# Staging four channels of both halves in two idle store tiles of a sliding-window kernel

## The chip, the cores and the metric

The kernel runs on one core of a Trainium2 chip. The metric is the device time of one execution in microseconds (us). All data is float32. The core has 16 DMA engines; DMAs are issued from the queues of SP (SyncE), ScalarE (ACT in the profile) and GpSimd (POOL in the profile). VectorE is DVE.

## The reference

The input x has shape (16, 64, 64, 64): batch, channel, row, column. The window is 8 by 8 with a stride of 4, so there are 15 by 15 windows. Each is cut out of all 64 channels:

```python
for i in range(n_h):                  # 15
    for j in range(n_w):              # 15
        result[:, i, j] = x[:, :, 4*i : 4*i + 8, 4*j : 4*j + 8]
```

The result has shape (16, 15, 15, 64, 8, 8). It is 58.98 MB, against 16.78 MB of input; nothing is computed, only copied.

## The kernel before, in words

**The input tile L.** The whole input lies in SBUF in one tile L of 128 partitions x (32 channels x 16 rows x 64 columns), 128 KB a partition. A partition is 64 * ch + 4 * b + q: half of the channels ch (0 or 1), batch b, row group q of 16 rows. One (channel, row group) of one batch is 4 KB in a row in memory. Partitions are also spoken of by y, the half of the batch: y = 0 is batches 0 to 7.

**The loads (L56 to L117).** `load(eng, ch, y, q, c0, c1)` fetches channels c0 to c1 of one half for one row group of eight batches: eight partitions, four apart, one 4 KB piece for each channel. The loop over y and q (eight steps) issues:

- on SP, first-half channels 4 to 32 for all eight steps (`HWP` = 8), each cut in two DMAs for the first five (`TWICE` = 5): 13 DMAs;
- on POOL, first-half channels 0 to 4 (`SMALL` = 4), then the second half, channels 0 to 32, or 8 to 32 where q = 0: 16 DMAs.

Ahead of the loop ScalarE issues one load (L106) of 16 partitions, all batches of q = 0: second-half channels 0 to 8 (`EC`).

**The index tiles (L69 to L101).** POOL and VectorE compute small tiles idx, idx_hi, idx_lo, idx_y with the row of the output that each partition goes to; this is over at 3.7 us.

**The store tiles.** Four tiles G0 to G3 of 128 partitions x 16 KB are used in turn (`tile_`). A partition of such a tile is one whole window: 64 channels x 8 x 8. Copies on ScalarE and VectorE gather windows out of L into a tile, then POOL issues an indirect DMA (`scatter`, L131) that writes 128 windows, 16 KB each, to their places in the output. Rows that fall outside are dropped by the bounds check.

- `part` (L182, copies in L189) fills a tile from one y alone, so it can start when half of the batches are loaded: eight copies of 32 partitions x 2048 elements. The first three tiles of the kernel are parts of y = 0, into G0, G1, G2.
- Then three parts of y = 1 alternate with `unit`s, which take both y and fill 64 partitions by each copy.
- `unit` with s > 0 makes windows that cross two row groups. There VectorE shifts the lower rows by one partition with a shuffle (L154).
- The last column is stored by two plain DMAs from SP (L238) out of partitions 32 to 96 of two tiles.

Waits between engines and the order of instructions on each engine are set by the framework from the data that they touch. In the program the loads stand ahead of all copies.

Of the kernel before, what the change touches and what calls it, by code (L numbers as in the profile page):

```python
# [10 lines left out]
def kernel(  # L11
# [7 lines left out]
    nc = tc.nc  # L19
    P = nc.NUM_PARTITIONS  # L20

    B, C, H, W = x.shape
    Bo, NH, NW, Co, WSo, WSo2 = out.shape
    WS = int(window_size)
# [3 lines left out]
    f32 = mybir.dt.float32  # L28
    i32 = mybir.dt.int32
    ALU = mybir.AluOpType  # L30
    CH = 2
    HQ = P // (B * CH)
    CL = C // CH
    RB = H // HQ
# [3 lines left out]
    HP = P // CH  # L38
    YB = 8
    NY = B // YB  # L40
    QP = YB * HQ
# [4 lines left out]
    gpool = ctx.enter_context(tc.tile_pool(name="gpool", bufs=1))  # L46


    L = lpool.tile([P, CL, RB, W], f32)
# [1 line left out]

    SMALL, HWP, TWICE = 4, 8, 5

    def load(eng, ch, y, q, c0, c1):  # L56
        p0 = ch * HP + y * QP + q
        eng.dma_start(out=L[p0 : p0 + QP - HQ + 1 : HQ, c0:c1, :, :], in_=x_v[ch, y, q, :, c0:c1, :])  # L58
# [42 lines left out]
    tt(idx_lo, idx_lo, th, ALU.add)  # L101


    EC = 8
    x_b = x.rearrange("b (ch cl) (hq r) w -> ch hq b cl (r w)", ch=CH, hq=HQ)
    nc.scalar.dma_start(out=L[HP : HP + (B - 1) * HQ + 1 : HQ, 0:EC, :, :], in_=x_b[1, 0, :, 0:EC, :])  # L106

    for y in range(NY):
        for q in range(HQ):
            hw = y * HQ + q < HWP  # L110
            if hw:
                mid = (SMALL + CL) // 2 if y * HQ + q < TWICE else CL
                load(nc.sync, 0, y, q, SMALL, mid)
                if mid < CL:
                    load(nc.sync, 0, y, q, mid, CL)
            load(nc.gpsimd, 0, y, q, 0, SMALL if hw else CL)
            load(nc.gpsimd, 1, y, q, EC if q == 0 else 0, CL)  # L117

    o_v = out.rearrange("b i j c r w -> (b i j) (c r w)")
    nxt = [min(p + 1, 31) for p in range(32)]  # L120
    NG = 4
    G = [gpool.tile([P, C, WS, WS], f32, name=f"G{n}") for n in range(NG)]

    o_q = out.rearrange("b i j c r w -> i j b (c r w)")

# [51 lines left out]
    def tile_():  # L177
        nonlocal at
        at += 1
        return G[(at - 1) % NG]  # L180

# [46 lines left out]
    for s in range(2):  # L228
        g = tile_()
        cols = slice(j * ST, j * ST + WS)  # L230
        for y in range(NY):
            d = slice(QP + y * QP, QP + (y + 1) * QP)
            for ch in range(CH):
                f = slice(ch * HP + y * QP, ch * HP + (y + 1) * QP)
# [39 lines left out]
```

## Time and profile before

| | |
|---|---|
| median of 3 runs | 188.5 us (188.49 to 189.4) |
| the profiled execution | 189.08 us, span 187.3 us |
| busy: VectorE, ScalarE, POOL | 142.5 us (76%), 139.3 us (74%), 45.0 us (24%) |
| DMA | 75.81 MB, mean 405 GB/s |
| queues' share of the 16 engines' time | POOL 84.6%, SP 12.8%, ScalarE 1.1% |
| HBM | 16.78 MB read, 62.91 MB written |

The span is the profiled execution from its first to its last instruction; the time of the run is 1.8 us longer. In the profile a line such as L189 is a line of the kernel's file; `G<-L` names what is written and read. The page's slices divide the span in 40 equal parts of 4.68 us; a DMA digit is the mean busy share of the 16 engines in tenths. Queue q0 is POOL's, q1 SP's, q10 ScalarE's. The "HBM written" counts also the rows that the bounds check drops; the DMA total does not.

### The profile page before, as it was taken

The page shows a single profiled execution, that of the slowest core. Times are in us where ns is not written, and L with a number is a line of the kernel's source. Part 1 is how long each engine was busy: PE and PEld are TensorE (multiplying, and loading weights), DVE is VectorE, ACT ScalarE, POOL GpSimd, SP SyncE. Part 2 cuts the span into 40 slices and gives each one's busy share as a digit, 9 for nine tenths or more (in the row PEclk, how much of TensorE's full clock was granted, in tenths as well). Part 3 has the DMA queues.
Part 4 walks back from the last instruction along what each step waited for, and adds up shares of the span by engine and source line. Part 5 has one row for each costly group of instructions (what it writes and reads, how often), then busy time and mean ns, then how long its engine had stood idle before and what let it go on. Part 6 is the DMA issues. An engine that isn't in the chain of part 4 may idle for free.

```text
span 187.3 us, 567 instructions
## 1 busy us (share of the span) xinstructions
DVE 142.5 (76%) x203; ACT 139.3 (74%) x94; POOL 45.0 (24%) x50
## 2 busy tenths in 40 slices
DVE  5000009998597969799999999999999999999600
ACT  0000009998599979988899999998999899989700
POOL 7411222207207050501222222112211121113000
DMA  5999999999999999999999999999999999999994
GB/s 127 295 402 400 400 400 398 399 400 419 421 427 437 425 427 423 441 413 434 434 420 432 422 434 413 441 430 420 434 416 436 406 437 409 420 423 406 441 420 206
DMA packets 10988, 75.81 MB, mean 405 GB/s; under 512 B 3288, under 2 KB 3288, under 8 KB 7384
## 3 DMA queue, kind: packets, MB, share of 16 engines
q0 software_dynamic: 8784, 65.81, 84.6%
q1 hardware_dynamic: 2056, 9.44, 12.8%
q10 hardware_dynamic: 144, 0.52, 1.1%
q14 instruction: 4, 0.03, 0.0%
HBM read 16.78 MB, written 62.91 MB: 425 GB/s over the span
## 4 chain that ended last, share of the span: by engine, by line
DMA 53%; DVE 28%; issue 6%; ACT 5%; POOL 2%; ACTq 1%; DVEq 0%; PEldq 0%
DMA L<-in_x_dram 20%; DMA out_dram<-G,idx_y 14%; DVE G L161 14%; DMA out_dram<-G,idx 13%; DVE G L154 9%; DMA out_dram<-G,idx_lo 6%; DVE G L189 4%; ACT G L236 3%; POOL L L58 2%; ACT G L151 1%; ACT G L165 1%; ACTq L269 1%; DVE G L151 0%; POOL pi L69 0%; DVEq L161 0%
## 5 line engine op out<-in xcount | busy, mean ns | idle before, releaser
L151 ACT COPY G<-L 64x2048 f32<-64x2048 f32 x46 | 87.2, 1896 | 5.1 <-DMA out_dram<-G,idx 2.9
L189 DVE COPY G<-L 32x2048 f32<-32x2048 f32 x30 | 36.7, 1224 | 29.9 <-DMA L<-in_x_dram 24.1
L161 DVE STREAM_SHUFFLE G<-L 64x1024 f32<-64x1024 f32 (+4 forms) x39 | 53.0, 1360 | 1.3
L154 DVE STREAM_SHUFFLE G<-L 64x1024 f32<-64x1024 f32 x30 | 38.4, 1281 | 0.0
L189 ACT COPY G<-L 32x2048 f32<-32x2048 f32 x18 | 33.9, 1896 | 4.1 <-DMA L<-in_x_dram 2.8
L189 ACT ACT_TABLE_LOAD x1 | 1.3, 1283 | 27.7 <-DMA L<-in_x_dram 27.7
L131 POOL DMA_INDIRECT out_dram<-G,idx_y x6 | 10.0, 1664 | 28.4 <-DVE G L189 27.4
L58 POOL DMA_DIRECT2D L<-in_x_dram x16 | 11.0, 700 | 22.2 <-DMA L<-in_x_dram 21.7
L131 POOL DMA_INDIRECT out_dram<-G,idx_lo x8 | 7.7, 961 | 30.6 <-DVE G L154 26.9
L131 POOL DMA_INDIRECT out_dram<-G,idx x8 | 9.2, 1152 | 17.8 <-DVE G L161 6.8
L131 POOL DMA_INDIRECT out_dram<-G,idx_hi x7 | 6.7, 960 | 27.0 <-DVE G L154 19.0
L165 ACT COPY G<-L 64x256 f32<-64x256 f32 (+2 forms) x21 | 10.2, 484 | 0.5
L151 DVE COPY G<-L 64x2048 f32<-64x2048 f32 x6 | 7.3, 1222 | 0.2
L236 ACT COPY G<-L 32x768 f32<-32x768 f32 x8 | 6.6, 830 | 0.1
L236 DVE COPY G<-L 32x1280 f32<-32x1280 f32 x8 | 6.5, 818 | 0.1
L161 DVE LOAD_MASK_SELECT G<-L x39 | 0.3, 9 | 1.2 <-DMA out_dram<-G,idx_y 0.9
L72 DVE TENSOR_SCALAR tb<-pi 128x1 int32<-128x1 int32 x1 | 0.2, 155 | 1.0 <-POOL pi L69 1.0
L166 DVE COPY G<-L 64x1280 f32<-64x1280 f32 x1 | 0.9, 876 | 0.0
L78 DVE TENSOR_TENSOR th<-tc,tq 128x1 int32<-128x1 int32 x2 | 0.3, 156 | 0.0
L75 DVE TENSOR_SCALAR th<-tc 128x1 int32<-128x1 int32 x2 | 0.3, 154 | 0.0
L69 POOL IOTA pi<- 128x1 int32 x1 | 0.1, 124 | 0.4 <-PEq L269 0.4
L78 DVE CUSTOM_DVE_ANT_0 idx<-tb,th 128x2 uint16<-128x2 uint16 x1 | 0.2, 160 | 0.0
(19 smaller groups left out, 2.7 us busy)
## 6 DMA issues: line engine op xcount, KB each, us to landing
L<-in_x_dram POOLq DMA_DIRECT2D x6, 1024.0 KB, 21.6
L<-in_x_dram SPq DMA_DIRECT2D x10, 448.0 KB
L<-in_x_dram SPq DMA_DIRECT2D x3, 896.0 KB
out_dram<-G SPq DMA_DIRECT2D x2, 1024.0 KB
L<-in_x_dram POOLq DMA_DIRECT2D x2, 768.0 KB, 17.9
L<-in_x_dram POOLq DMA_DIRECT2D x8, 128.0 KB, 21.5
L<-in_x_dram ACTq DMA_DIRECT2D x1, 512.0 KB
out_dram<-G,idx POOLq DMA_INDIRECT x8, 12.8
```

What stands on the lines that cost most here:

```text
L58: eng.dma_start(out=L[p0 : p0 + QP - HQ + 1 : HQ, c0:c1, :, :], in_=x_v[ch, y, q, :, c0:c1, :])
L75: nc.vector.tensor_scalar(out=d[:, :], in0=a[:, :], scalar1=float(m), scalar2=None, op0=ALU.mult)
L78: nc.vector.tensor_tensor(out=d[:, :], in0=a[:, :], in1=b[:, :], op=op)
L131: st = nc.gpsimd.indirect_dma_start(out=o_v, out_offset=bass.IndirectOffsetOnAxis(ap=ix[:, 0:1], axis=0), in_=g.rearrange("p c r w -> p (c ...
L151: copy(out=g[d, cs, :, :], in_=L[f, :, s * ST : s * ST + WS, cols])
L154: nc.vector.stream_shuffle(out=g[d, cs, ST:WS, :], in_=L[f, :, 0:ST, cols], mask=nxt)
L161: nc.vector.stream_shuffle(out=out, in_=in_, mask=same)
L165: act(out=out[:, 0:k], in_=in_[:, 0:k])
L166: other(out=out[:, k:], in_=in_[:, k:])
L189: (act if (2 * d + ch) % 3 == 0 else dve)(out=g[d * QP : (d + 1) * QP, ch * CL : (ch + 1) * CL, :, :], in_=L[f : f + QP, :, s * ST : s * S ...
L236: copy(out=g[d, ch * CL + c0 : ch * CL + c1, :, :], in_=L[f, c0:c1, s * ST : s * ST + WS, cols])
L269: with _tile.TileContext(nc) as tc:
```

## The change

Four channels (`FC` = 4) of both halves no longer go straight into L. A store tile's 16 KB a partition hold just four channels of 16 x 64 elements, and G2 and G3 are not used as store tiles at first, so they are viewed as staging tiles S[0] and S[1]. ScalarE issues four loads for the first half and SP four for the second, one for each q. Each takes all 16 batches into 16 partitions, four apart, between partitions 32 and 95. Then four copies, two on ScalarE (first half) and two on VectorE (second half), bring channels 0 to 4 into L, one y at a time.

The direct loads begin at channel 4 instead of 0. SP takes first-half channels 8 to 32 for the first six steps (`HWP` = 6), each in one DMA; POOL takes first-half channels 4 to 8 for these and 4 to 32 for the last two steps, and second-half channels 4 to 32 for all. The early load of eight channels on ScalarE (`EC`) is gone, and so is the cut of SP's loads in two (`TWICE`).

```diff
-    SMALL, HWP, TWICE = 4, 8, 5
+    SMALL, HWP = 4, 6
...
-    EC = 8
+    NG = 4
+    G = [gpool.tile([P, C, WS, WS], f32, name=f"G{n}") for n in range(NG)]
+    FC = C * WS * WS // (RB * W)
+    S = [g.rearrange("p c r w -> p (c r w)").rearrange("p (c r w) -> p c r w", c=FC, r=RB) for g in G[NG - CH :]]
     x_b = x.rearrange("b (ch cl) (hq r) w -> ch hq b cl (r w)", ch=CH, hq=HQ)
-    nc.scalar.dma_start(out=L[HP : HP + (B - 1) * HQ + 1 : HQ, 0:EC, :, :], in_=x_b[1, 0, :, 0:EC, :])
+    for ch in range(CH):
+        for q in range(HQ):
+            s = S[ch][QP + q : QP + q + (B - 1) * HQ + 1 : HQ]
+            (nc.scalar, nc.sync)[ch].dma_start(out=s, in_=x_b[ch, q, :, 0:FC, :])
 
     for y in range(NY):
         for q in range(HQ):
             hw = y * HQ + q < HWP
             if hw:
-                mid = (SMALL + CL) // 2 if y * HQ + q < TWICE else CL
-                load(nc.sync, 0, y, q, SMALL, mid)
-                if mid < CL:
-                    load(nc.sync, 0, y, q, mid, CL)
-            load(nc.gpsimd, 0, y, q, 0, SMALL if hw else CL)
-            load(nc.gpsimd, 1, y, q, EC if q == 0 else 0, CL)
+                load(nc.sync, 0, y, q, FC + SMALL, CL)
+            load(nc.gpsimd, 0, y, q, FC, FC + SMALL if hw else CL)
+            load(nc.gpsimd, 1, y, q, FC, CL)
+
+    for y in range(NY):
+        for ch in range(CH):
+            f = slice(QP + y * QP, QP + (y + 1) * QP)
+            d = slice(ch * HP + y * QP, ch * HP + (y + 1) * QP)
+            (nc.scalar.copy, nc.vector.tensor_copy)[ch](out=L[d, 0:FC, :, :], in_=S[ch][f])
```

More of the change, by code (lines that the diff above doesn't have):

```diff
@@ L111 @@
             if hw:
-                mid = (SMALL + CL) // 2 if y * HQ + q < TWICE else CL
-                load(nc.sync, 0, y, q, SMALL, mid)
-                if mid < CL:
-                    load(nc.sync, 0, y, q, mid, CL)
-            load(nc.gpsimd, 0, y, q, 0, SMALL if hw else CL)
-            load(nc.gpsimd, 1, y, q, EC if q == 0 else 0, CL)
+                load(nc.sync, 0, y, q, FC + SMALL, CL)
[6 more added lines that the diff above has]
+            (nc.scalar.copy, nc.vector.tensor_copy)[ch](out=L[d, 0:FC, :, :], in_=S[ch][f])
     o_v = out.rearrange("b i j c r w -> (b i j) (c r w)")
     nxt = [min(p + 1, 31) for p in range(32)]
-    NG = 4
-    G = [gpool.tile([P, C, WS, WS], f32, name=f"G{n}") for n in range(NG)]
     o_q = out.rearrange("b i j c r w -> i j b (c r w)")
```

## The prediction

> **What bounds the kernel now.** I read the page first (busy time and the rows in slices), then the windows over the first 60 us, the DMA queues of single stretches, the waits, and the timeline around the first stores. The two DMA rows of the page:
>
> ```profile
> DMA  5999999999999999999999999999999999999994
> GB/s 127 295 402 400 400 400 398 399 400 419 421 427 437 425 427 423 441 413 434 434 420 432 422 434 413 441 430 420 434 416 436 406 437 409 420 423 406 441 420 206
> ```
>
> A slice is 4.68 us. All 16 DMA engines are busy from the second slice to the last. While the input is read (4 KB packets) they move 400 GB/s, while windows are stored (16 KB packets) about 425. So 75.81 MB through 16 full engines is the bound, and only bytes that move earlier can shorten it: the first two slices (127 and 295) are the one place with room. The windows (busy us per engine, clock, DMA share, GB/s) show that place:
>
> ```profile
> 0.00:2.00 2.00, 0.91 (x9) 0.00 (x0) 0.84 (x6) 1.00 0.00 0
> 2.00:4.00 2.00, 1.43 (x11) 0.00 (x0) 2.00 (x4) 1.00 0.87 231
> 4.00:6.00 2.00, 0.00 (x0) 0.00 (x0) 2.00 (x5) 1.00 0.84 209
> 6.00:8.00 2.00, 0.00 (x0) 0.00 (x0) 0.47 (x1) 1.00 0.96 340
> 8.00:10.00 2.00, 0.00 (x0) 0.00 (x0) 0.55 (x1) 1.00 0.96 313
> 20.00:28.00 8.00, 0.23 (x1) 0.30 (x1) 1.88 (x4) 1.00 1.04 400
> ```
>
> From 2 to 10 us, 2.19 MB move; at 400 GB/s it would be 3.20. The 1.01 MB missing are 2.5 us. The queues of three stretches (2 to 4, 16 to 32, 45 to 47 us; packets, MB, share of 16 engines) say who moves them:
>
> ```profile
> q10 hardware_dynamic: 114, 0.45, 83.5%
> q1 hardware_dynamic: 3, 0.01, 3.0%
> ```
> ```profile
> q0 software_dynamic: 1690, 3.54, 58.5%
> q1 hardware_dynamic: 741, 2.84, 45.2%
> ```
> ```profile
> DMA packets 288, 0.84 MB, mean 420 GB/s; under 512 B 155, under 2 KB 155, under 8 KB 264
> q0 software_dynamic: 204, 0.51, 64.8%
> q1 hardware_dynamic: 84, 0.33, 40.0%
> ```
>
> q10 is ScalarE's queue, q1 SP's, q0 POOL's. ScalarE's one load (16 partitions, one per batch) alone fills 83.5% of 16 engines, so it runs on all of them. SP's loads (8 partitions) never fill more than 45.2%, 7.2 engines: they sit on eight ("half A"). POOL's share then fits the other eight ("half B", its second-half channels) plus its small first-half loads on A. At 45 to 47 us SP still loads while POOL's queue has 288 - 264 = 24 packets over 8 KB in flight, which are stores: half A ends its loads later than half B.
>
> The compute engines, from the waits and the timeline:
>
> ```profile
> ACT L189 <- DMA L<-in_x_dram: 27.7, 1, 27.7
> DVE G L189 <- DMA L<-in_x_dram: 24.1, 1, 24.1
> ```
> ```profile
> 27.70 1.28 ACT L189 ACT_TABLE_LOAD   x1 [27.70 <-DMA L<-in_x_dram]
> 27.77 1.32 POOL L58 DMA_DIRECT2D L<-in_x_dram  x1 [0.62 <-DMA L<-in_x_dram]
> 42.67 1.38 POOL L131 DMA_INDIRECT out_dram<-G,idx_y  x1 [8.49 <-DVE G L189]
> ```
>
> ScalarE and VectorE have nothing to do until 27.7 us. The first store is issued at 42.67, before the loads end, so the engines never run dry. Later VectorE is nearly full too (29.55 of 30 us busy from 108 to 138), but a store lands 10.1 to 12.8 us after its issue (medians of the page's DMA issues by offset tile), where 2.1 MB need 4.9 at 425 GB/s: some 5 us are queued ahead, so the engines stay the bound.
>
> **The change, part by part.** Bytes first. The staged loads are 8 of 16 partitions x 4 channels x 4 KB = 0.262 MB, 2.10 MB in all, over 16 engines. SP's direct loads fall from 7.34 MB to 6 x 8 x 24 x 4 KB = 4.72. POOL's second-half loads fall from 7.86 to 7.34 MB, its first-half ones grow from 1.05 to 2.62 (the last two row groups of first-half channels move from SP to POOL). The sum stays 16.78 MB.
>
> *Balance.* Half A before: 7.34 + 1.05 + half of ScalarE's 0.52 = 8.65 MB; after: 4.72 + 2.62 + 1.05 = 8.39, the same as half B. The 0.26 MB less are 1.3 us at 200 GB/s for eight engines. Between 0 (if B's lead is already used up by the stores that follow) and 1.3 us; I take half, 0.65.
>
> *Start.* Now nothing is on q1 until 4 us, and POOL's packets come after that; from 2 us on, both hardware queues would hold 16-engine loads. Lower bound: their packets take what ScalarE's took from 2 to 4 us (83.5% x 32 engine-us / 114 = 234 ns, 280 GB/s on 16 engines), until 2.10 MB are through at 9.5 us. Add about 0.2 MB of POOL's by 10 us: 2.30 MB against 2.19, 0.3 us. Upper bound: 280 GB/s until 5 us, then 400 with the packets of later (45.2% x 256 / 741 = 156 ns): 0.84 + 2.00 = 2.84 MB, 0.65 MB more, 1.5 us at 425. ScalarE's load has the same shape, so nearer to the lower end: 0.55 us.
>
> [...]
>
> *Copies.* ScalarE gets two copies of 32 x 4096 elements. Its 32x2048 copy takes 1896 ns, so 3.8 us each, 7.6 together; VectorE's takes 1224 ns, so 2.45 each, 4.9 together. The staged loads land by about 9.5 to 11 us (2.10 MB at 231 to 280 GB/s from 2 us), so the copies end by 19 us, under the wait that lasts to 27.7: cost nothing. Without that cover it is 7.6 us of ScalarE ahead of the first store. The table load (1.28 us) moves under the same wait, so the first store may come 1.3 us earlier; it is worth nothing while the engines are full. VectorE's copies come beside POOL's load issues. Those last 0.54 to 0.66 us on their own and 1.32 and 1.14 (27.77, 33.04 us) beside VectorE's copies; two such delays of 0.66 us hide behind POOL's queued loads, which land 21.6 us (median) after issue.
>
> *Waits and queues.* On SP four staged loads stand ahead of everything, some 0.7 us of issue each (2.8 us). Already now SP waits three times for a load to land before it can issue the next (1.3 us in total, L58); with eight more landings ahead of them all six direct loads may wait so. Behind them stands only the pair of last stores at 173 us; who waits is half A, with SP's staged loads still running to 9 us. I count nothing, at most 0.5 us loss. ScalarE issues four loads instead of one, 0.64 us each, in idle time. The first three store tiles are G0, G1, G2, so the third waits for the staging copies of G2, long done.
>
> Sum: 0.65 + 0.55 = 1.2 us off, with bounds of 0.5 loss and 2.8 gain. The profiled execution took 189.08 us (span 187.3 and 1.8 outside it), the median 188.5: 187.9 for a profiled run, 187.3 for the median.
>
> **Rivals.** *No change.* The staged loads crawl at 234 ns a packet or longer, SP's direct loads start late behind their landings, and half B's earlier finish is already used by stores. For: ScalarE's load is the slow one of the trace, and the queues share their engines. Against: half A is still loading at 45 to 47 us. Gain 0 to 0.5, about 188.2 us. [...]
>
> *Slower: the first store comes after the loads have ended.* The new copies stand on ScalarE ahead of the first tile's. If they don't run under the 27.7 us (because the staged loads, which share the queues, land late, or the copies wait for the direct loads too), up to 7.6 us come on top: the first store at 42.67 - 1.28 + 7.6 = 49.0, its packets 2 us later (now issued at 42.67, first 16 KB packet of the trace at 44.7) at 51, with loads over at about 46. The engines stand empty for 5 us; less the 1.2 it is +3.8, 192.3 us. With only the second pair late (3.8 us) packets come at 47.2, a hole of 1.2, about 188.5. It decides from a first store later than about 44 us. For: ScalarE's nine copies are already a chain of 17 us from 29 us to the stores. Against: 27.7 us of idle time for 7.6 us of work. Middle 190.5.
>
> *Faster still.* Both terms at their upper ends, 2.8 us: 185.7.
>
> **How the numbers follow.** Forecast 187.3 (186.7 to 187.9): 0.45. Faster still: 0.08. No change: 0.22. Late first store: 0.25. What a measurement of this kernel can tell is about 0.5%, 0.94 us: under 187.56 counts as faster, over 189.44 as slower. Of the forecast 0.40 lies under it, with 0.08 it makes 0.48. The forecast's other 0.05 and no change make 0.27; the late store's 0.25 is the chance of slower. The range, 185.8 to 190.8, holds all but the last tenth of the fast case and the worst part of the late store.
>
> **What would show it.** Right: the second slice at 340 GB/s or more; q10 and q1 on all engines from 2 us; the staging copies done before 20 us; first window copies still near 27 us; first store before 44 us; the DMA row without a digit under 9 from the second slice on. Wrong: slices of 280 GB/s up to 10 us (no change), or a hole in the DMA row near 45 us (late store). A table load still at 27 us would show that the copies had no cover.

## The result, and the profile after

The changed kernel takes 187.88 us (median of 20 runs, 187.09 to 188.88), the kernel before 188.8 (20 runs, 188.49 to 189.4). The ratio is 0.9951, 95% interval 0.9937 to 0.9964: 0.9 us faster, clear of zero, and just short of the 0.5% (0.94 us) that the prediction set as its bound for "faster". The forecast was a gain of 1.2 us. The profiled execution took 187.89 us (span 186.1) against 189.08 (187.3), 1.2 us less; but the one of the kernel before lies 0.3 us above the median of that kernel.

The page's two DMA rows:

```profile
DMA  5999999999999999999999999999999999999994
GB/s 165 359 402 403 399 401 400 381 385 424 433 440 423 431 433 430 433 430 433 424 435 419 433 426 423 433 412 433 398 444 396 444 419 409 440 409 433 409 447 204
```

The engines are still full from the second slice to the last. The first two slices have gone from 127 and 295 to 165 and 359 GB/s. Two slices between 33 and 42 us have become lower (381, 385, before 399, 400). In the windows (engines' busy us, clock, DMA share, GB/s):

```profile
2.00:4.00 2.00, 1.43 (x11) 0.00 (x0) 2.00 (x4) 1.00 0.85 250
4.00:6.00 2.00, 0.00 (x0) 0.00 (x0) 2.00 (x5) 1.00 1.05 369
6.00:8.00 2.00, 0.00 (x0) 0.00 (x0) 0.97 (x2) 1.00 0.98 353
8.00:10.00 2.00, 0.00 (x0) 0.00 (x0) 0.00 (x0) 1.00 1.03 371
28.00:42.00 14.00, 13.26 (x11) 13.42 (x8) 1.30 (x1) 1.00 1.04 389
```

From 4 to 6 us it was 209 GB/s, now 369. The queues from 2 to 4 us and from 45 to 47 us:

```profile
q10 hardware_dynamic: 86, 0.29, 55.7%
q1 hardware_dynamic: 57, 0.21, 29.7%
```
```profile
DMA packets 333, 0.87 MB, mean 437 GB/s; under 512 B 246, under 2 KB 246, under 8 KB 291
q0 software_dynamic: 333, 0.87, 109.8%
```

SP's queue moves 57 packets before 4 us instead of 3. At 45 to 47 us q1 has nothing left, and 291 - 246 = 45 packets of 4 KB still come through POOL's queue, where it was 264 - 155 = 109 on both queues before: less than half as much is left to load. Which half of the engines the 45 are for, the profile does not say. The timeline:

```profile
4.08 13.30 SPq L58 DMA_DIRECT2D L<-in_x_dram  x6
10.83 1.28 ACT L126 ACT_TABLE_LOAD   x1 [10.83 <-DMA G<-in_x_dram]
11.82 4.60 DVE L126 COPY L<-G 32x4096 f32<-32x4096 f32 x2 [8.17 <-DMA G<-in_x_dram]
12.13 7.23 ACT L126 COPY L<-G 32x4096 f32<-32x4096 f32 x2
14.59 2.60 POOL L58 DMA_DIRECT2D L<-in_x_dram  x2 [7.62 <-DMA L<-in_x_dram]
28.47 16.98 ACT L196 COPY G<-L 32x2048 f32<-32x2048 f32 x9 [9.11 <-DMA L<-in_x_dram]
42.14 1.40 POOL L138 DMA_INDIRECT out_dram<-G,idx_y  x1 [9.72 <-ACT G L196]
```

L126 are the staging copies: over at 19.4 us, 9 us before ScalarE's first window copy at 28.47. The first store is issued at 42.14, half a microsecond earlier than before.

The loads that ScalarE's first window copy waits for landed 0.8 us later than before (28.47 us, before 27.70). The copy still starts earlier, because the table load (1.28 us) is now done under the earlier wait, at 10.83. In the kernel before it stood between the landing and this copy:

```profile
29.00 16.98 ACT L189 COPY G<-L 32x2048 f32<-32x2048 f32 x9
```

### The profile page after: what moved, and what is told of

Same layout as the page of the kernel before. It is cut to its first block, busy times and chain, and to the rows that moved or that the text cites. A ratio compares the mean times of both kernels' runs of the same rounds, so it can differ in the third digit from the quotient of the medians.

```text
span 186.1 us, 575 instructions
## 1 busy us (share of the span) xinstructions
DVE 146.8 (79%) x205; ACT 146.5 (79%) x96; POOL 47.7 (26%) x50
## 4 chain that ended last, share of the span: by engine, by line
DMA 41%; DVE 37%; issue 8%; ACT 5%; POOL 2%; ACTq 1%; POOLq 0%; DVEq 0%; PEldq 0%
DVE G L168 16%; DMA out_dram<-G,idx 14%; DMA out_dram<-G,idx_y 13%; DMA L<-in_x_dram 13%; DVE G L161 11%; DVE G L196 10%; ACT G L243 3%; POOL L L58 2%; ACT G L158 1%; ACT G L172 1%; ACTq L276 0%; DVE G L158 0%; POOLq L138 0%; POOL pi L69 0%; POOL out_dram L138 0%
## 5 line engine op out<-in xcount | busy, mean ns | idle before, releaser
L196 DVE COPY G<-L 32x2048 f32<-32x2048 f32 x30 | 36.6, 1220 | 14.9 <-DMA L<-in_x_dram 12.1
L138 POOL DMA_INDIRECT out_dram<-G,idx_y x6 | 10.7, 1776 | 26.7 <-DVE G L196 16.3
L58 POOL DMA_DIRECT2D L<-in_x_dram x16 | 11.9, 760 | 19.5 <-DMA L<-in_x_dram 19.0
L138 POOL DMA_INDIRECT out_dram<-G,idx x8 | 10.4, 1295 | 18.1 <-ACT G L158 9.3
L126 DVE COPY L<-G 32x4096 f32<-32x4096 f32 x2 | 4.6, 2284 | 8.2 <-DMA G<-in_x_dram 8.2
L126 ACT COPY L<-G 32x4096 f32<-32x4096 f32 x2 | 7.2, 3604 | 0.0
```

What stands on the lines that cost most here:

```text
L126: (nc.scalar.copy, nc.vector.tensor_copy)[ch](out=L[d, 0:FC, :, :], in_=S[ch][f])
L138: st = nc.gpsimd.indirect_dma_start(out=o_v, out_offset=bass.IndirectOffsetOnAxis(ap=ix[:, 0:1], axis=0), in_=g.rearrange("p c r w -> p (c ...
L196: (act if (2 * d + ch) % 3 == 0 else dve)(out=g[d * QP : (d + 1) * QP, ch * CL : (ch + 1) * CL, :, :], in_=L[f : f + QP, :, s * ST : s * S ...
```

## The experiments

Two theories stood against each other for the gain. "Start": the lead in bytes that the loads win in the first 10 to 20 us is all. "Balance": the fuller half of the DMA engines sets the end, and its 0.26 MB less are the gain. A third question was what the staging is for, since 16-partition loads could go straight into L. Each row of this table is one kernel. Each ratio is against runs of the kernel before that were taken beside it. The last three columns are from the profile: what had moved by 20 us, when the first store was issued, and the time from there to the end of the span.

| kernel | median us | ratio to before (95%) | MB by 20 us | first store, us | span after it, us |
|---|---|---|---|---|---|
| before | 188.8 | 1 | 6.25 | 42.67 | 144.6 |
| after | 187.88 | 0.9951 (0.9937 to 0.9964) | 6.75 | 42.14 | 144.0 |
| bal | 188.43 | 0.9976 (0.9967 to 0.9985) | 6.46 | 42.44 | 144.4 |
| noec | 189.36 | 1.0027 (1.0018 to 1.0036) | 6.11 | 43.42 | 144.0 |
| hwp8 | 188.28 | 0.9970 (0.9959 to 0.9982) | 6.63 | 42.40 | 144.3 |
| copies2 | 188.06 | 0.9953 (0.9935 to 0.9971) | 6.65 | 42.38 | 144.2 |
| copies3 | 193.58 | 1.0253 (1.0237 to 1.0269) | 6.70 | 47.55 | 144.1 |
| direct | 191.57 | 1.0143 (1.0128 to 1.0158) | 5.79 | 45.96 | 143.9 |
| stage0 | 192.17 | 1.0176 (1.0161 to 1.0192) | 5.11 | 46.41 | 144.0 |
| stride8 | 191.16 | 1.0128 (1.0098 to 1.0157) | 5.61 | 45.14 | 144.0 |
| unbal | 191.96 | 1.0173 (1.0151 to 1.0195) | 5.96 | 45.89 | 144.3 |
| actall | 191.05 | 1.0112 (1.0093 to 1.0131) | 6.49 | 45.15 | 144.2 |

**bal: even bytes, little else.**

```diff
-    EC = 8
+    EC = 4
-    nc.scalar.dma_start(out=L[HP : HP + (B - 1) * HQ + 1 : HQ, 0:EC, :, :], in_=x_b[1, 0, :, 0:EC, :])
+    for ch in range(CH):
+        nc.scalar.dma_start(out=L[ch * HP : ch * HP + (B - 1) * HQ + 1 : HQ, 0:EC, :, :], in_=x_b[ch, 0, :, 0:EC, :])
...
+                c0 = EC if q == 0 else 0
-                load(nc.sync, 0, y, q, SMALL, mid)
+                load(nc.sync, 0, y, q, c0 + SMALL, mid)
...
-            load(nc.gpsimd, 0, y, q, 0, SMALL if hw else CL)
+            load(nc.gpsimd, 0, y, q, c0, c0 + SMALL if hw else CL)
```

> The kernel before, with only the bytes of the two halves evened out: ScalarE's early load is cut in two, four channels of the first half and four of the second (q = 0), SP and POOL begin at channel 4 there. Half A 8.39 MB instead of 8.65, as in the changed kernel; no staging, no copies, SP's 8-partition loads as before. Theory 'balance' (the fuller half sets the end): 1.3 us less than before, about 187.5, the last load landing 1 us or more earlier than 48.8. Theory 'start' (the lead is won between 2 and 10 us by loads that run on all 16 engines): no change, 188.8 within 0.3, 273 GB/s from 2 to 10 us as before. As predicted (half of it): 188.1.

It gained 0.24%, 0.45 us: neither 1.3 nor 0. The last 4 KB packet of a load did end earlier, at 46.44 us instead of 48.12, but the time did not follow it. And the start changed as well. With the early load in two halves SP's first packet came at 2.94 us instead of 3.89; by 20 us 0.21 MB more had moved, which is 0.5 us at 425 GB/s. So the lead alone would account for the gain. What is left for balance is no more than the scatter of such a start between single executions (about 0.1 MB or 0.2 us, see hwp8).

**noec: even bytes, poorer start.**

```diff
-    nc.scalar.dma_start(out=L[HP : HP + (B - 1) * HQ + 1 : HQ, 0:EC, :, :], in_=x_b[1, 0, :, 0:EC, :])
...
-            load(nc.gpsimd, 1, y, q, EC if q == 0 else 0, CL)
+            load(nc.gpsimd, 1, y, q, 0, CL)
```

> The kernel before without ScalarE's early load (EC = 0): POOL loads second-half channels 0 to 32 for q = 0 too. Bytes of the halves are even (8.39 MB each), as in the run 'bal', but the start is poorer: until POOL's first packet only SP's eight engines work. Theory 'balance': faster than before, at least the 0.45 us of 'bal', 188.3 or less. Theory 'start': MB moved by 10 us decide, not the balance; with eight engines idle from 2 to 5 us 0.1 to 0.2 MB less than the 2.19 of before, 189.0 to 189.3.

Its windows from 2 to 6 us:

```profile
2.00:4.00 2.00, 1.43 (x11) 0.00 (x0) 2.00 (x4) 1.00 0.40 121
4.00:6.00 2.00, 0.00 (x0) 0.00 (x0) 2.00 (x5) 1.00 0.74 236
```

Without ScalarE's load 0.40 of the engines are busy from 2 to 4 us, where it was 0.87 before. The kernel is 0.27% slower than before though its halves are even by the prediction's count. So between the two theories it speaks for the start: an effect of the balance by itself is not seen.

**unbal: a failed test of the same question.**

```diff
-            (nc.scalar, nc.sync)[ch].dma_start(out=s, in_=x_b[ch, q, :, 0:FC, :])
+            if ch == 1 and q >= 2:
+                for y in range(NY):
+                    p0 = (1 + y) * QP + q
+                    nc.sync.dma_start(out=S[1][p0 : p0 + QP - HQ + 1 : HQ], in_=x_v[1, y, q, :, 0:FC, :])
+            else:
+                (nc.scalar, nc.sync)[ch].dma_start(out=s, in_=x_b[ch, q, :, 0:FC, :])
```

> The changed kernel, with two of SP's four staged loads cut into 8-partition loads, which all fall on half A: half A 8.65 MB and half B 8.13 again, as before the change; six of eight staged loads still run on all 16 engines. Theory 'balance': the gain is lost, about 188.8. Theory 'start': most of it stays, 188.0 to 188.2, with about 2.6 MB moved by 10 us.

It lost 3.2 us against before, more than either theory allows, so it says nothing on balance. The cut loads do something else:

```profile
10.00:20.00 10.00, 4.58 (x2) 8.49 (x3) 2.68 (x2) 1.00 1.04 340
```

The engines are full (1.04) and slow: 340 GB/s where the changed kernel has 406. Half of the cut rows lie in partitions 64 to 95, to which SP's direct loads never write. It may be the effect of the next three runs, brought in unasked; for this run that is argued, not shown. The first store also came late, at 45.89 us, and the engines were not full then (DMA share 0.96 from 46 to 60 us, 1.01 in the changed kernel).

**direct, stage0, stride8: what the staging is for.** First the same eight loads straight into L, with no copies:

```diff
-            s = S[ch][QP + q : QP + q + (B - 1) * HQ + 1 : HQ]
+            s = L[ch * HP + q : ch * HP + q + (B - 1) * HQ + 1 : HQ, 0:FC]
...
-    for y in range(NY):
-        for ch in range(CH):
-            f = slice(QP + y * QP, QP + (y + 1) * QP)
-            d = slice(ch * HP + y * QP, ch * HP + (y + 1) * QP)
-            (nc.scalar.copy, nc.vector.tensor_copy)[ch](out=L[d, 0:FC, :, :], in_=S[ch][f])
```

> The changed kernel without staging: the same eight 16-partition loads go straight into L (first half into partitions 0 to 63, second half into 64 to 127), the four copies are gone, all else is the same. Theory 'shape of the loads': the number of partitions per load matters and the place does not: 187.9 as the changed kernel, 369 GB/s from 4 to 6 us. Rival 'place': partitions 32 to 95 were needed; then the packets of q10 and q1 take over 230 ns and 2 to 8 us runs at 230 to 290 GB/s: 188.5. The copies themselves cost nothing in both.

Then staging kept, its rows moved:

```diff
-            s = S[ch][QP + q : QP + q + (B - 1) * HQ + 1 : HQ]
+            s = S[ch][q : q + (B - 1) * HQ + 1 : HQ]
...
-            f = slice(QP + y * QP, QP + (y + 1) * QP)
+            f = slice(y * QP, (y + 1) * QP)
```

> The changed kernel with the staging rows moved from partitions 32 to 95 of the two store tiles to partitions 0 to 63; the same loads, queues, memory rows and copies. Theory 'place' (16 engines whose rows lie within one block of 64 partitions hinder each other, as in the run 'direct', where all packets took 225 ns from 4 to 12 us): as slow as 'direct' or slower, since now both queues' loads fall into the same 64 partitions: 2 to 10 us at 220 to 290 GB/s, 191.5 or more. Rival 'L' (it is loads into L beside other loads into L that hinder each other, not the partitions): as the changed kernel, 187.9.

And the rows spread over all 128 partitions:

```diff
-            s = S[ch][QP + q : QP + q + (B - 1) * HQ + 1 : HQ]
+            s = S[0][ch * HQ + q : ch * HQ + q + (B - 1) * 2 * HQ + 1 : 2 * HQ]
...
-            (nc.scalar.copy, nc.vector.tensor_copy)[ch](out=L[d, 0:FC, :, :], in_=S[ch][f])
+            (nc.scalar.copy, nc.vector.tensor_copy)[ch](out=L[d, 0:FC, :, :], in_=S[0][f])
```

> The changed kernel with the staging rows eight partitions apart in one store tile: each load's 16 rows lie in partitions 8 b + r from 0 to 127, r = 0 to 3 for the first half's loads and 4 to 7 for the second's. The copies read the same number of rows, so four channels of L get rows of other batches; all else is the same. [...] Rival '64-partition block' (it is enough that a load's rows lie in both halves of the partitions): 160 to 180 ns, 187.9 as the changed kernel.

In stride8 the result is no longer the reference's, since four channels of L hold rows of other batches; it is here for its times alone. The DMA queues from 4 to 12 us of the changed kernel, of direct, of stage0 and of stride8, in this order:

```profile
DMA packets 1175, 3.00 MB, mean 376 GB/s; under 512 B 442, under 2 KB 442, under 8 KB 1175
q10 hardware_dynamic: 234, 0.76, 27.0%
```
```profile
DMA packets 898, 2.24 MB, mean 280 GB/s; under 512 B 352, under 2 KB 352, under 8 KB 898
q10 hardware_dynamic: 238, 0.78, 36.2%
```
```profile
DMA packets 712, 1.83 MB, mean 229 GB/s; under 512 B 265, under 2 KB 265, under 8 KB 712
q10 hardware_dynamic: 219, 0.73, 42.1%
```
```profile
DMA packets 819, 2.09 MB, mean 261 GB/s; under 512 B 310, under 2 KB 310, under 8 KB 819
q10 hardware_dynamic: 228, 0.76, 37.9%
```

The same memory rows, the same queues, almost the same number of packets on q10; the partitions differ, and in direct the copies are gone too. The 0.76 MB of q10 are 186 packets of 4 KB, the others have 4 bytes. A 4 KB packet so takes 27.0% x 128 engine-us / 186 = 186 ns in the changed kernel, and in the same way 243 in direct (the expectation of stage0 has 225 there), 301 in stage0 and 262 in stride8. In direct the staged loads of the two queues write to 64 partitions each, in stage0 both to the same 64: 280 and 229 GB/s. So for this rate it is not L and not the copies, it is the place. Stride8 decides how to say it: its loads reach both halves of the partitions and are no faster than direct's. Its rate was 261 GB/s and its time 191.16 us, with 262 ns a packet where the rival said 160 to 180. So it is not enough that a load's rows lie in both halves. What else the places differ in, no run here shows.

The time of direct, 191.57 us, is not the price of the place alone: without the staging copies ScalarE's table load stands behind the landing again (1.28 us from 30.98 on), and ScalarE's first window copy comes after it, at 32.28.

Which engine writes which row no run here shows. The two halves of the balance are an estimate from shares of time: in the kernel before, SP's queue had 45.2% of the 16 engines from 16 to 32 us and 46.6% from 4 to 6 us.

**hwp8: the dip at 28 to 42 us.**

```diff
-    SMALL, HWP = 4, 6
+    SMALL, HWP = 4, 8
```

> The changed kernel with HWP = 8: SP takes first-half channels 8 to 32 for all eight steps, so its queue lasts to the end of the loads; bytes on both halves as in the changed kernel. In the changed kernel the stretch 28 to 42 us runs at 389 GB/s where before it was 398. Theory 'SP ran out': after SP's last load (36.6 us) half A works off POOL's many 4-byte packets with nothing beside them; with HWP = 8 the stretch is back at 398, 0.13 MB or 0.3 us gained: 187.6. Rival 'the dip has another cause' (stores, copies): no change, 187.9.

The dip is gone, as the theory said:

```profile
28.00:42.00 14.00, 12.99 (x11) 13.16 (x7) 1.49 (x1) 1.00 1.04 399
```

The time is not better: 188.28 us, against 187.88. In this profile 6.63 MB had moved by 20 us instead of 6.75, with the same first loads, so the starts of single executions differ by about 0.1 MB (copies2: 6.65, copies3: 6.70). What the mended dip is worth lies within this scatter. The edit does two things at once: SP's queue no longer runs empty, and POOL's last two first-half loads shrink from 28 channels to four (from 36 to 42 us 333 packets under 512 B, 722 in the changed kernel). That the work moved to POOL makes the dip is shown; which of the two does it, and that it costs time, is not.

**copies2 and copies3: the cover of the copies, and the slower rival made real.**

```diff
-    for y in range(NY):
+    for y in (0, 1, 0, 1):        # copies3: (0, 1) * 3
         for ch in range(CH):
             f = slice(QP + y * QP, QP + (y + 1) * QP)
```

> The changed kernel with the four staging copies issued twice. ScalarE's then end near 12.1 + 14.4 = 26.5 us, under the wait for the loads that lasts to 28.5. Theory 'covered': no change from the changed kernel, 187.9. Rival 'VectorE's copies hold up POOL's load issue and that costs': each costs POOL more delay, 188.2 or more.

> The changed kernel with the four staging copies issued three times: ScalarE's end near 33.8 us, 5.3 us after the loads of the first tiles landed (28.5). This brings on the mishap of the prediction's slower rival. Theory 'late first store': first store near 47.4 instead of 42.1, its packets near 49.5, the halves' loads over at 44.8 and 46.0: a hole of 3.5 to 4.7 us, 191 to 192.5. Rival 'still room' (some 5 us of stores are queued ahead later, so the delay is absorbed): 188.0 to 188.5.

Copies2 has about the ratio of the changed kernel (0.9953, 0.9951): 7.2 us more of ScalarE and 4.6 of VectorE cost nothing under the wait. Copies3's ScalarE timeline, first store and slices:

```profile
12.10 21.75 ACT L126 COPY L<-G 32x4096 f32<-32x4096 f32 x6
33.88 22.76 ACT L196 COPY G<-L 32x2048 f32<-32x2048 f32 x12
47.55 1.49 POOL L138 DMA_INDIRECT out_dram<-G,idx_y  x1 [14.59 <-ACT G L196]
```
```profile
DMA  5999999995699999999999999999999999999995
GB/s 169 355 402 402 400 396 403 382 388 208 274 438 433 410 414 438 414 434 409 414 431 426 404 434 417 438 404 417 438 428 398 428 421 428 428 400 434 434 424 212
```

The first store comes at 47.55 us (expected 47.4) and the DMA row has its first hole, 5 and 6 tenths. Slices 10 and 11 move 208 and 274 GB/s instead of 424 and 433; a slice of this span is 4.79 us, so (216 + 159) x 4.79 us = 1.80 MB are missing, 4.2 us at 425 GB/s. The kernel lost 5.7 us against the changed one. Of the other 1.5 some lies in slower stores afterwards (420 GB/s from 80 to 170 us, 424 in the changed kernel: 0.8 us); the rest is open.

**actall: one queue for all staged loads.**

```diff
-            (nc.scalar, nc.sync)[ch].dma_start(out=s, in_=x_b[ch, q, :, 0:FC, :])
+            nc.scalar.dma_start(out=s, in_=x_b[ch, q, :, 0:FC, :])
```

> The changed kernel with all eight staged loads on ScalarE's queue, so that SP's direct loads are first in their own queue and fill half A while ScalarE's loads fill both halves. Theory 'start' (MB moved by 10 us decide; the changed kernel has 2.67 against 2.18 of before): a gain over 187.9 only if more than 2.7 MB are moved by 10 us; at most 0.3 us, 187.6. Rival: the staged loads take twice as long on one queue, the copies end later (near 24 us) and still under the wait, no change: 187.9.

Neither time came true: 191.05 us, slower than before, although 2.41 MB had moved by 10 us (before 2.19) and 6.49 by 20 us (before 6.25). Its timeline:

```profile
17.80 4.85 POOL L58 DMA_DIRECT2D L<-in_x_dram  x2 [8.20 <-DMA L<-in_x_dram]
31.47 22.75 ACT L196 COPY G<-L 32x2048 f32<-32x2048 f32 x12 [11.12 <-DMA L<-in_x_dram]
45.15 1.60 POOL L138 DMA_INDIRECT out_dram<-G,idx_y  x1 [8.27 <-ACT G L196]
```

The staged loads of the second half land late: VectorE's staging copies start at 17.92 us, not at 11.82. POOL's loads land later too: those issued from 4 to 12 us take 25.1 us (896 KB) and 25.9 us (128 KB), in the changed kernel 20.0 and 20.9. The window copies start at 31.47 instead of 28.47. The first store is issued at 45.15, and the slice around 45 us falls to 316 GB/s. This is the prediction's slower rival again, by another way: not the copies but the loads under them came late.

**A third account: the first store.** The last two columns of the table point to an explanation that none of these runs was made to test. In all twelve profiles the first store comes 13.7 us after the start of ScalarE's first window copy, and the span ends 143.9 to 144.6 us after the first store. The bytes that are left to move at that store differ by more: 59.02 MB in copies3, 60.52 before, which is 3.5 us at 425 GB/s. VectorE is about as full as the DMA engines in this part. A window of the kernel before (VectorE, ScalarE and POOL busy, clock, DMA share, GB/s):

```profile
108.00:138.00 30.00, 29.55 (x45) 28.78 (x22) 6.56 (x7) 1.00 1.00 425
```

From 80 to 160 us VectorE is busy for 78.5 of 80 us, before the change and after it. So behind the first store the pace may be VectorE's and not that of the DMA engines. Then the time follows the first store, and early bytes count only as far as they bring it forward.

For the slow kernels this fits better than the lead. At 20 us direct, stride8 and stage0 are 0.46, 0.64 and 1.14 MB behind, worth 1.1, 1.5 and 2.7 us; they lose 2.7, 2.4 and 3.3 us, and their first stores come 3.3, 2.5 and 3.7 us later. For the faster ones the lead fits the size better: bal, hwp8, copies2 and the changed kernel gain 0.45 to 0.92 us, with first stores only 0.23 to 0.53 us earlier. In the changed kernel the 0.53 us come from the table load, since the loads themselves landed later. The kernel before with nothing but the table load moved forward would part the two accounts. There is no such run, so which of them makes the gain of 0.9 us is open.

## Why the prediction was right

The time was near (187.3 forecast, 187.88 measured), and the early rate rose as the prediction said it would. But the sum was put together wrongly: one term came out near nothing, another larger than forecast, and that they added up to nearly the right time is in part luck. Both terms rest on the sentence "so the engines stay the bound", and the first store brings that into doubt: that the early rate makes the gain fits, but is not shown.

- **Balance, 0.65 us: this term was mis-sized, about 0.** Less is left to load late (45 packets of 4 KB instead of 109 at 45 to 47 us), but noec is slower than before with even halves, and bal's gain is no larger than its lead in bytes. The lower end, 0, is the one that fits; that B's lead is used up by the stores is not shown.
- **Start, 0.55 us: mis-sized the other way.** From 2 to 10 us 2.68 MB moved instead of 2.19, and the lead at 20 us is 0.50 MB, 1.2 us at 425 GB/s if all of it reached the end; the whole gain was 0.9. I leaned to the lower bound because ScalarE's old load has the same shape and its packets were slow (234 ns). Shape was the wrong thing to match: that load wrote to partitions 64 to 127, the staged ones to 32 to 95, and from 4 us on the place decides, as direct, stage0 and stride8 show (280, 229 and 261 GB/s from 4 to 12 us, against 376). From 2 to 4 us the staged packets on ScalarE's queue were no faster than the old load's: counted as packets of 4 KB, 55.7% x 32 engine-us / 71 = 251 ns against 83.5% x 32 / 110 = 243. On SP's queue they took 29.7% x 32 / 52 = 183 ns. The 156 ns of the upper bound have SP's 4-byte packets counted in; for its 693 packets of 4 KB they are 167.
- **Copies: right, but for the table load.** Two of 3604 ns on ScalarE and two of 2284 on VectorE (forecast 3.8 and 2.45 us), over at 19.4 us (forecast 19), and free even when doubled. The two POOL issues beside VectorE's copies took 1.3 us each; no loss from them is seen. The table load did move under the wait, and the first store came 0.5 us earlier where 1.3 was allowed for. That this "is worth nothing while the engines are full" is not shown, and the last column of the table speaks against it: the time after the first store is the same within 0.8 us in all twelve profiles.
- **SP's waits: no loss is seen.** It waits four times for a staged load, 2.6 us in all, and issues its direct loads from 4.08 us on; q1's longest pause between packets before 10 us is 0.3 us, at 4.5 us.
- **The 28 to 42 us stretch was not foreseen.** 9 GB/s less over 14 us are 0.13 MB, 0.3 us; SP's last packet of a load ends at 36.6 us.
- **Rivals.** No change is out by the interval, though by little. The late first store did not happen. Of its point of decision, 44 us, the runs show only that 43.42 (noec) costs 0.5 us and 45.14 or later 2.1 us and more, the latter also where the DMA row has no hole (stride8, direct, stage0). Copies3 gave 193.6 where the rival said up to 192.3. The gain is not one of more queues, since both kernels issue from the same three. What changed is that both hardware queues start with loads of 16 partitions.

## What to carry to other kernels

Where the DMA engines look full to the end, write down two numbers for every variant: the megabytes moved by an early fixed time, and the time of the first store. The nine kernels here without a hole at the first store come in the order of their lead at 20 us, and all twelve in the order of their first store, each but for pairs whose intervals overlap. When two such numbers move together, make a run that moves only one. Try other partitions for the rows of a load: the same loads ran at 229 to 376 GB/s. Where the final layout forbids the good ones, staging in an idle buffer and copying under a wait was free here as long as the copies ended before that wait did (ratio 0.9953 in copies2 with twice the copies, 0.9951 in the changed kernel). A first store that came 2.5 us later or more cost about as much in every run here: 2.5 to 4.9 us later, 2.1 to 4.8 us lost.

## What I had not expected of the hardware

The partitions to which a 16-row load writes changed the rate of everything in flight: 376 GB/s in the changed kernel from 4 to 12 us, 280, 261 and 229 with the same loads at other partitions. The packets of the other queues slow down with them: in the same stretch POOL's queue q0 moved 0.89 MB in the changed kernel, 0.49 in direct and 0.37 in stage0, which is 30.7%, 25.1% and 22.0% of 128 engine-us, or 181, 269 and 312 ns for each 4 KB. The second is the stretch from 36 to 42 us in the changed kernel, when SP's queue is done and POOL's is alone: 722 packets under 512 B came through and 381 GB/s, where it was 306 and 400 before, and 333 and 400 in hwp8. Whether the many small packets or the missing second queue cost the rate is not shown.
